# Triangular inverses in blocks of 8, and vector work handed to GpSimd and ScalarE, in a decoder trunk on one core

## The chip, the cores and the metric

One core of a Trainium2 chip. The metric is the device time of one execution in microseconds (us). The engines are PE (TensorE; PEld its weight loads), DVE (VectorE), ACT (ScalarE), POOL (GpSimd) and SP (SyncE, which here only issues transfers). Each engine works through its own instructions in the order in which the program holds them; an instruction that waits holds up all behind it on that engine.

## The reference, cut to what matters

One layer of a hybrid decoder: 2064 prompt tokens (16 learned ones and 2048) and 8 short sample sequences pass through one wide input projection, a gated delta rule (8 heads of 128), an RWKV-7 recurrence (16 heads of 64), two output projections, a gated merge and a last projection. Both recurrences are computed in chunks of 64 tokens. For each chunk and head the kernel needs the inverse of a unit lower triangular 64x64 matrix:

```
lower = where(strict, einsum('bnhik,bnhjk->bnhij', k_beta, k) * decay, 0)
t_inv = triangular_solve(eye + lower, eye, left_side=True, lower=True)
u = einsum('bnhij,bnhjv->bnhiv', t_inv, v_beta)
...
v_new = u_c - w_c @ s ;  o = (q_c * exp(gc)) @ s + qk_c @ v_new
s = s * exp(g_last) + k_tail^T @ v_new          # chunk after chunk
```

## The kernel before, in words

The 33 chunks are cut into 5 segments of 6, 6, 7, 7 and 7 chunks. A segment has 12 units, 4 pairs of delta-rule heads (G) and 8 pairs of RWKV heads (R), so there are 60 units in all. A unit projects its columns (`proj`: 24 matmuls a column block, with each fp32 operand split into a high part and a low rest, both of type fp32r), prepares its chunk matrices (`g_g2`, `g_r2`), inverts them (`g_inv`) and walks through its chunks (`g_g3`, `g_r3`).

`g_inv` goes in two steps. The diagonal 16x16 blocks of all chunks of a unit (48 or 56 of them, one to a partition) are sent through DRAM (`ex`) into the tile `iM`. A second tile, `iD`, is filled with identities by a transfer from `in_consts`. DVE then solves the blocks row by row: row i needs a product of i x i elements into `iT` and a sum along it into row i of `iD`, 15 rows, 30 instructions that each need the one before. GpSimd copies the transpose, the blocks go back through DRAM (`bk`) into `Dn` and `Dt`, and PE combines the 16x16 blocks to 64x64 (`ps_n`, `Z`). `iM`, `iD` and `iT` have one buffer each.

Weights: on first use (segment 0 and the first microseconds of the next), `w_half` loads 128x512 raw weights (`wr`), ACT casts the high part (`wh`), and DVE or GpSimd, in turn by half, subtracts for the rest (`wl`); both parts are stored in DRAM and only loaded from there later on. `split` does the same to an activation before a sum over partitions (`colsum`): `sh` is the high copy and `sl` the rest.

The order of all instructions is made by the kernel itself before anything runs. It records every operation with its dependencies and a planned cost, and a list scheduler (`Sched`) plays a plan in which each engine takes its ready operation of highest rank (`pick`: the chunk walk first, then what touches PSUM, then the rest). `replay` writes that order out, so every instruction carries the source line of `replay` (L903 before, L905 after), and tiles tell them apart. The plan is not corrected at run time: where a transfer lands later than planned, the instruction that needs it stands where the plan put it and its engine stands with it.

Of the kernel before, what the change touches and what calls it, by code (L numbers as in the profile page):

```python
# [4 lines left out]
F32 = mybir.dt.float32  # L5
# [3 lines left out]
ALU = mybir.AluOpType  # L9
AX = mybir.AxisListType  # L10
# [3 lines left out]
D = 1024  # L14
# [11 lines left out]
TS = 4  # L26
NS = NSEQ * TS
SEGMAX = 7
NT = 30
ND = 24  # L30
INFLIGHT = 5
# [10 lines left out]
CONST_LAYOUT = {}  # L42
# [85 lines left out]
def plan(seq):  # L128
    nch = (seq + NM + 63) // 64
    nseg = (nch + SEGMAX - 1) // SEGMAX  # L130
    base, extra = divmod(nch, nseg)
    segs, c0 = [], 0
    pad = nch * 64 - seq - NM
    for i in range(nseg):
        n = base + (1 if i >= nseg - extra else 0)
        t0, t1 = c0 * 64, (c0 + n) * 64
        p = max(0, pad - t0)
        segs.append(dict(i=i, nch=n, T=n * 64, pad=p, nreal=n * 64 - p, r0=max(t0 - pad, 0), last=False, smp=(i == 0)))
        c0 += n
    segs[-1]["last"] = True  # L140
    return segs
# [764 lines left out]
class Trunk:  # L906
# [55 lines left out]
    def split(self, x, n):  # L962

        h, l = self.tr("sh"), self.tr("sl")
        self.nc.vector.tensor_copy(h[:, :n], x)
        self.tt(l[:, :n], x, h[:, :n].bitcast(F32), ALU.subtract)
        return h, l

# [14 lines left out]
    def w_half(self, key):  # L983


        sync = self.nc.sync
        v = lambda x: x.rearrange("p (k n) -> p k n", n=128)
        wh, wl = self.w_tile(F32R, "wh"), self.w_tile(F32R, "wl")
        if key in self.w_dr:
            for w, d in zip((wh, wl), self.w_dr[key]):  # L990
                sync.dma_start(w.bitcast(F32), v(d))
        else:
            raw = self.w_tile(F32, "wr")
            sync.dma_start(raw, v(self.I["wt"][key[0], key[1]]))
            self.nc.scalar.copy(wh, raw)
            self.tt(wl, raw, wh.bitcast(F32), ALU.subtract, self.nc.gpsimd if key[1] else self.nc.vector)
            self.w_dr[key] = [self.p_dr.tile([128, 512], F32, name=f"w{q}_{key[0]}_{key[1]}", tag=f"w{q}_{key[0]}_{key[1]}") for q in "hl"]
            for w, d in zip((wh, wl), self.w_dr[key]):
                sync.dma_start(v(d), w.bitcast(F32))
        return wh, wl  # L1000
# [23 lines left out]
    def setup(self):  # L1024
        nc, I = self.nc, self.I
        P = self.p_c
        nc.scalar.preload_act_table_set("natural_log_exp_and_others")
        self.eps = P.tile([128, 4], F32, name="eps")
        nc.vector.memset(self.eps[:, 0:1], EPS)
        nc.vector.memset(self.eps[:, 1:2], GN_EPS)  # L1030
        nc.vector.memset(self.eps[:, 2:3], 1.0)
        nc.vector.memset(self.eps[:, 3:4], -2.4260151319598084)
        self.consts = P.tile([128, CONST_ON], F32, name="consts")
        nc.sync.dma_start(self.consts[:, 0:128], I["consts"][:, 0:128])

    def g_setup(self):
        nc, I = self.nc, self.I
        P = self.p_c
# [43 lines left out]
        self.abd = [self.dr([128, 8, 40], "abd") for _ in range(2)]  # L1082
        nc.sync.dma_start(self.abd[0], abH.bitcast(F32))
        nc.sync.dma_start(self.abd[1], abL.bitcast(F32))
        self.wbd = [P.tile([128, 2, 128], F32, name=f"wbd{i}") for i in range(1)]
        self.xo = [P.tile([128, 2, 64], F32, name=f"xo{i}") for i in range(2)]
        for w in self.wbd + self.xo:
            nc.gpsimd.memset(w, 0.0)
        self.GS = [P.tile([128, 128], F32, name=f"gs{h}") for h in range(8)]
# [279 lines left out]
    def g_inv(self, sg, u):  # L1369

        nc = self.nc
        n = sg["nch"]
        ex, Nt = u.pop("ex"), u.pop("Nt")
        NB = 8 * n
        M = self.p_i.tile([128, 16, 16], F32, tag="iM", name="iM", bufs=1)
        nc.sync.dma_start(M[:NB], ex)
        Dk = self.p_i.tile([128, 2, 16, 16], F32, tag="iD", name="iD", bufs=1)
        io = CONST_LAYOUT["ID16"][0]
        nc.sync.dma_start(Dk[:NB, 0].rearrange("p a b -> p (a b)"), self.I["consts"][:NB, io:io + 256])
        yield  # L1380
        nc.vector.tensor_scalar(M[:NB], M[:NB], -1.0, None, ALU.mult)
        tmp = self.p_i.tile([128, 16, 16], F32, tag="iT", name="iT", bufs=1)
        for i in range(1, 16):
            a = M[:NB, 0:i, i].unsqueeze(1).to_broadcast([NB, i, i])
            b = Dk[:NB, 0, 0:i, 0:i].rearrange("p m c -> p c m")
            self.tt(tmp[:NB, 0:i, 0:i], a, b, ALU.mult)
            nc.vector.tensor_reduce(Dk[:NB, 0, i, 0:i], tmp[:NB, 0:i, 0:i], AX.X, ALU.add)
            if i % 4 == 3:
                yield
        nc.gpsimd.tensor_copy(Dk[:NB, 1], Dk[:NB, 0].rearrange("p a b -> p b a"))  # L1390
        yield
        bk = self.dr([8 * n, 2, 16, 16], "bk")
        nc.sync.dma_start(bk, Dk[:NB])
        for w, dst in ((0, self.Dn), (1, self.Dt)):
            d3 = dst.rearrange("p (c i) -> p c i", i=64)
            for hf in range(2):
                for b in range(4):
                    q = (hf * 4 + b) * n
                    r = hf * 64 + b * 16
                    nc.sync.dma_start(d3[r:r + 16, 0:n, 16 * b:16 * b + 16], bk[q:q + n, w].rearrange("c j i -> j c i"))  # L1400
        yield
        T = n * 64

        c3 = lambda x: x[:, 0:T].rearrange("p (c t) -> p c t", t=64)

        def quad(lhs, rhs, j=0):

            ps = self.ps("n")
            for c in range(n):
                for hf in range(2):  # L1410
                    r = slice(64 * hf, 64 * hf + 64)
                    k = slice(64 * c + j, 64 * c + 64)
                    self.mm(ps[r, k], lhs[r, 64 * c:64 * c + 64], rhs[r, k])
            return ps

        ps = quad(Nt, self.Dn)
        yield
        Wp = self.t("Wp")
        nc.scalar.copy(Wp[:, :T], ps[:, :T])
        Z = self.t("Z")  # L1420
        nc.gpsimd.tensor_copy(c3(Z)[:, :, 0:16], c3(self.Dt)[:, :, 0:16])
        yield

        for it in range(1, 4):
            j = 16 * it
            ps = quad(Wp, self.Dt if it == 1 else Z, j)
            yield
            self.tt(c3(Z)[:, :, j:], c3(self.Dt)[:, :, j:], c3(ps)[:, :, j:], ALU.subtract)
            yield
        u["U"] = Z  # L1430


    def g_g2(self, sg, p, u):
        nc = self.nc
        T, last, n = sg["T"], sg["smp"], sg["nch"]
        h0 = 2 * p
        W = T + (NS if last else 0)
        GT, cv = sg["GT"], u["cv"]
# [4 lines left out]
        E3 = EP[:, 0:T].rearrange("p (c t) -> p c t", t=64)  # L1443
# [7 lines left out]
        for hh in range(2):  # L1451
            EG = self.t("EG")
            nc.sync.dma_start(EG[:, 0:W], sg["gcd"][h0 + hh:h0 + hh + 1, 0:W].to_broadcast([128, W]))
            sq = {}
# [15 lines left out]
            self.act(EG[:, :W], EG[:, :W], AF.Exp)  # L1470
            if hh == 0:

                self.tt(E3, E3, GT[:, :n, p].unsqueeze(2).to_broadcast([128, n, 64]), ALU.subtract)
                self.tt(E3, E3, self.cst("MNEG").unsqueeze(1).to_broadcast([128, n, 64]), ALU.add, nc.gpsimd)
                self.act(EP[:, 0:T], EP[:, 0:T], AF.Exp)
            yield
            gl = self.sm([128, SEGMAX + 8], "gl", 6)
# [4 lines left out]
            for si, kind in enumerate("kq"):  # L1482
                x = cv[kind, hh]
# [16 lines left out]
        for c0 in range(0, n, 4):  # L1500
            m = min(4, n - c0)
# [23 lines left out]
        for c0 in range(0, n, 4):  # L1525
            m = min(4, n - c0)
# [9 lines left out]
    def g_g3(self, sg, p, u):  # L1536
        nc = self.nc
# [6 lines left out]
        for c in range(n):  # L1544
            k = slice(64 * c, 64 * c + 64)
            g = self.ps("g")
            pr, po, pc = g[:, 0:128], g[:, 128:256], g[:, 256:512]
            for hh in range(2):
                self.mm(pr[H[hh]], kt["k", hh][:, k], S[hh])
            yield  # L1550
            R = self.sm([128, 128], "gR")
            self.tt(R, vt[:, c], pr, ALU.subtract)
            yield
            for hh in range(2):
                self.mm(pr[H[hh]], U[H[hh], k], R[H[hh]])
            yield
            w = self.wbd[0]
            nc.scalar.copy(w[H[0], 0], pr[H[0]])
            nc.vector.tensor_copy(w[H[1], 1], pr[H[1]])
            yield  # L1560
            for hh in range(2):
                self.mm(po[H[hh]], kt["q", hh][:, k], S[hh], start=True, stop=False)
                self.mm(po[H[hh]], KE[:, c, 1], w[:, hh], start=False, stop=True)
            nc.cut(False)
            self.mm(pc, ktl[:, c], w.rearrange("p h v -> p (h v)"))
            yield
            for hh in range(2):
                self.stt(S[hh], S[hh], u["gl", hh][:, c:c + 1], pc[:, 128 * hh:128 * hh + 128], ALU.mult, ALU.add)
            nc.scalar.copy(oS3[:, c], po)
            sq = self.sm([128, 128], "osq", 1)  # L1570
            self.act(sq, oS3[:, c], AF.Square, accum_out=rs[:, c:c + 1])
            yield
# [4 lines left out]
        for c0 in range(0, n, 4):  # L1577
            m = min(4, n - c0)
# [350 lines left out]
    def g_r3(self, sg, p, u):  # L1929
# [5 lines left out]
        H = [slice(0, 64), slice(64, 128)]  # L1935
        AL = u["AL"]
        y = self.t("y")
        xo = self.xo[p % 2]

        nc.scalar.copy(X[H[0], 0, 0], S[H[0]])  # L1940
        nc.vector.tensor_copy(X[H[1], 0, 1], S[H[1]])
# [399 lines left out]
```

## Time and profile before

| | |
|---|---|
| median of 3 runs (lowest, highest) | 4353.93 us (4351.48, 4364.67) |
| profiled execution, its own time | 4371.86 us |
| its span (first to last instruction) | 4370.1 us |
| PE busy | 4066.9 us, 93% |
| DVE busy | 2726.3 us, 62% |
| ACT busy | 1965.2 us, 45% |
| POOL busy | 992.3 us, 23% |
| mean granted TensorE clock | 0.941 |

The profiled execution took 17.9 us more than the median of the runs. Busy time is the union of an engine's instructions; the rest of the span it stood idle. The granted clock is the share of full speed that TensorE was allowed, 1.0 or 0.5 at any moment. Most instructions come from one line, so groups are read by tile: `iT<-iM,iD` writes tile iT from iM and iD.

### The profile page before, as it was taken

What the parts mean: (1) busy time and instruction counts of PE and PEld (TensorE: products, weight loads), DVE (VectorE), ACT (ScalarE), POOL (GpSimd) and SP (SyncE); (2) the same over time, 40 slices, a digit from 0 to 9 for tenths busy, and PEclk for the clock granted to TensorE, in tenths of its full rate; (3) what the DMA queues carried; (4) which work ended last, traced back from release to release, by engine and by line L of the source; (5) the groups of instructions that cost most, each with busy time, mean ns of one, the idle gap of its engine ahead of it and who ended that gap; (6) DMA issues with size and microseconds to landing.
All of it is one profiled execution on the core that took longest, in us unless ns stands there. A gap on an engine that the chain in (4) does not pass through costs nothing. (4 is left out here: it accounts for less than half of the span.)

```text
span 4370.1 us, 91290 instructions
## 1 busy us (share of the span) xinstructions
PE 4066.9 (93%) x32684; PEld 3485.0 (80%) x32684; DVE 2726.3 (62%) x7052; ACT 1965.2 (45%) x4842; POOL 992.3 (23%) x1972
## 2 busy tenths in 40 slices
PE   6888999888999999999999999998998999999998
PEld 6767777778888888888788889787887887778887
DVE  6888677756576754557666645676763456666622
ACT  6544444525444443445444433554443334554431
POOL 3434233413121121212212121121121112111210
PEclk9889788979999999999999999999999999999999
DMA  7636465758745456864445567544445775444467
GB/s 254 201 117 203 136 199 172 243 171 279 235 145 154 137 166 211 263 201 148 126 127 157 172 223 261 159 139 131 128 151 170 237 239 151 128 140 137 143 221 256
DMA packets 660688, 790.09 MB, mean 181 GB/s; under 512 B 251105, under 2 KB 347209, under 8 KB 660234
## 3 DMA queue, kind: packets, MB, share of 16 engines
q1 hardware_dynamic: 660234, 784.25, 57.5%
q8 instruction: 259, 4.24, 0.4%
q14 instruction: 195, 1.60, 0.1%
HBM read 602.29 MB, written 180.56 MB: 179 GB/s over the span
## 5 line engine op out<-in xcount | busy, mean ns | idle before, releaser
L903 PE MATMUL ps_p<-hHL,wh 128*128 128x448 f32 (+3 forms) x7760 | 1828.1, 373 | 30.7 <-ACT wh L903 10.3
L903 PEld LDWEIGHTS ps_p<-hHL,wh 128*128 128x128 f32 x7760 | 1421.3, 195 | 156.1 <-issue 28.3
L903 PE MATMUL ps_p<-hHL,wl 128*128 128x448 f32 (+3 forms) x3880 | 911.6, 358 | 4.9 <-DVE wl L903 2.9
L903 PEld LDWEIGHTS ps_p<-hHL,wl 128*128 128x128 f32 x3880 | 730.2, 193 | 39.0 <-DVE wl L903 3.7
L903 POOL COPY xo<-X 64x64 f32<-64x64 f32 x528 | 172.4, 327 | 809.6 <-ACT X L903 380.1
L903 DVE TENSOR_TENSOR iT<-iM,iD 56x1 f32<-56x1 f32 (+1 forms) x900 | 295.5, 328 | 75.0 <-DMA iD<-in_consts 58.5
L903 ACT COPY raw<-ps_p 128x448 f32<-128x448 f32 (+3 forms) x285 | 144.2, 506 | 343.2 <-PE ps_p L903 313.8
L903 DVE SCALAR_TENSOR_TENSOR cv<-raw,pv,cv 128x448 f32<-128x448 f32 (+1 forms) x360 | 259.3, 720 | 56.0 <-ACT cv L903 48.6
L903 DVE TENSOR_REDUCE iD<-iT 56x1 f32<-56x1 f32 (+1 forms) x900 | 205.1, 228 | 17.7
L903 POOL TENSOR_TENSOR wl<-wr,wh 128x512 fp32r<-128x512 f32 x105 | 149.0, 1419 | 212.0 <-ACT wh L903 137.5
L903 ACT ACTIVATE X<-ps_c 64x64 f32<-64x64 f32 x264 | 55.5, 216 | 289.0 <-PE ps_c L903 124.2
L903 ACT CAST wh<-wr 128x512 fp32r<-128x512 f32 x210 | 128.3, 613 | 77.6 <-DMA wr<-in_wt 21.8
L903 ACT ACTIVATE X<-ps_c,dc 64x64 f32<-64x64 f32 x224 | 68.7, 307 | 207.2 <-DVE X L903 106.4
L903 DVE TENSOR_SCALAR X<-ps_c,dc 64x64 f32<-64x64 f32 x224 | 64.9, 291 | 135.0 <-PE ps_c L903 98.0
L903 ACT ACTIVATE sig<-cv 128x448 f32<-128x448 f32 (+2 forms) x120 | 67.3, 561 | 177.7 <-DVE cv L903 175.9
L903 PE MATMUL ps_p<-mhl,wh 128*128 128x448 f32 (+2 forms) x640 | 141.5, 359 | 5.7 <-ACT wh L903 4.5
L903 DVE TENSOR_SCALAR X<-ps_c 64x64 f32<-64x64 f32 x264 | 58.8, 227 | 131.1 <-PE ps_c L903 88.9
L903 DVE TENSOR_TENSOR Z<-Dt,ps_n 128x336 f32<-128x336 f32 (+1 forms) x180 | 66.9, 372 | 115.5 <-PE ps_n L903 100.0
L903 PE MATMUL ps_g<-gs,cv 128*64 128x128 f32 x1056 | 122.2, 308 | 17.0 <-DVE wbd L903 8.4
L903 PEld LDWEIGHTS ps_n<-Z,Wp 64*64 64x64 f32 x3168 | 109.9, 143 | 24.8 <-issue 9.5
L903 PE MATMUL ps_a<-RH,LH 64*128 64x128 f32 x1056 | 129.3, 292 | 0.0
L903 PE MATMUL ps_n<-Z,Wp 64*64 64x16 f32 (+1 forms) x3168 | 120.3, 220 | 7.7 <-DVE Z L903 5.8
(337 smaller groups left out, 7444.1 us busy)
## 6 DMA issues: line engine op xcount, KB each, us to landing
wh<-wh SPq DMA_DIRECT2D x1050, 256.0 KB
wl<-wl SPq DMA_DIRECT2D x1050, 256.0 KB
wr<-in_wt SPq DMA_DIRECT2D x210, 256.0 KB
gl<-gt SPq DMA_DIRECT2D x72, 224.0 KB
gt<-gt SPq DMA_DIRECT2D x48, 224.0 KB
xt<-in_x_prompt SPq DMA_DIRECT2D x29, 256.0 KB
xt<-in_x_prompt SPq DMA_DIRECT2D x13, 512.0 KB
out_y_p<-xt SPq DMA_DIRECT2D x26, 256.0 KB
```

Source lines behind the costliest of these rows:

```text
L903: getattr(getattr(nc, eng), name)(*[g(x) for x in a], **{q: g(x) for q, x in k.items()})
```

## The change

- `g_inv` solves the two diagonal 8x8 blocks of each 16x16 block side by side, in 7 rows instead of 15, and gets the 8x8 block below them from two matrix products, each in two halves of 256 elements (product into `iT`, sum into the new tile `iX` or into `iD`): 22 DVE instructions instead of 30.
- The identity in `iD` is written by two memsets on GpSimd; the 60 transfers from `in_consts` are gone.
- The negation of `iM`, which is the first to wait for the transfer from `ex`, goes from DVE to GpSimd, as a multiplication by a column of -1.
- In `g_g2` the first operation on `EP` (which waits for a transfer) goes from DVE to GpSimd, and the second, of the same size, from GpSimd to DVE.
- `w_half` subtracts on GpSimd for every half: 105 subtractions of 128x512 change from DVE to GpSimd.
- `split` makes the high copy on ACT: 240 casts change from DVE to ACT.
- `SMP`, `NXO` and `NWB` name numbers that keep their values.

```diff
     def split(self, x, n):
-        self.nc.vector.tensor_copy(h[:, :n], x)
+        self.nc.scalar.copy(h[:, :n], x)
...
-            self.tt(wl, raw, wh.bitcast(F32), ALU.subtract, self.nc.gpsimd if key[1] else self.nc.vector)
+            self.tt(wl, raw, wh.bitcast(F32), ALU.subtract, self.nc.gpsimd)
...
-        nc.sync.dma_start(Dk[:NB, 0].rearrange("p a b -> p (a b)"), self.I["consts"][:NB, io:io + 256])
+        nc.gpsimd.memset(D0, 0.0)
+        nc.gpsimd.memset(D0[:, 0:256:17], 1.0)
         yield
-        nc.vector.tensor_scalar(M[:NB], M[:NB], -1.0, None, ALU.mult)
+        self.tt(M, M, self.eps[:NB, 4:5].unsqueeze(2).to_broadcast([NB, 16, 16]), ALU.mult, nc.gpsimd)
-        for i in range(1, 16):
-            a = M[:NB, 0:i, i].unsqueeze(1).to_broadcast([NB, i, i])
-            b = Dk[:NB, 0, 0:i, 0:i].rearrange("p m c -> p c m")
-            self.tt(tmp[:NB, 0:i, 0:i], a, b, ALU.mult)
-            nc.vector.tensor_reduce(Dk[:NB, 0, i, 0:i], tmp[:NB, 0:i, 0:i], AX.X, ALU.add)
+        for i in range(1, 8):
+            for_a = M2[:, :, 0:i, i].unsqueeze(2).to_broadcast([NB, 2, i, i])
+            for_b = D2[:, :, 0:i, 0:i].rearrange("p h m c -> p h c m")
+            tv = tmp[:NB, 0:2, 0:i, 0:i]
+            self.tt(tv, for_a, for_b, ALU.mult)
+            nc.vector.tensor_reduce(D2[:, :, i, 0:i], tv, AX.X, ALU.add)
...
+        for q in range(2):
+            tv = tmp[:NB]
+            self.tt(tv, M[:, 0:8, 8 + 4 * q:12 + 4 * q].rearrange("p m i -> p i m").unsqueeze(2).to_broadcast([NB, 4, 8, 8]),
+                    D[:, 0:8, 0:8].rearrange("p m c -> p c m").unsqueeze(1).to_broadcast([NB, 4, 8, 8]), ALU.mult)
+            nc.vector.tensor_reduce(Xt[:NB, 4 * q:4 * q + 4], tv, AX.X, ALU.add)
...
+        for q in range(2):
+            tv = tmp[:NB]
+            self.tt(tv, D[:, 8 + 4 * q:12 + 4 * q, 8:16].unsqueeze(2).to_broadcast([NB, 4, 8, 8]),
+                    Xt[:NB].rearrange("p m c -> p c m").unsqueeze(1).to_broadcast([NB, 4, 8, 8]), ALU.mult)
+            nc.vector.tensor_reduce(D[:, 8 + 4 * q:12 + 4 * q, 0:8], tv, AX.X, ALU.add)
...
-                self.tt(E3, E3, GT[:, :n, p].unsqueeze(2).to_broadcast([128, n, 64]), ALU.subtract)
-                self.tt(E3, E3, self.cst("MNEG").unsqueeze(1).to_broadcast([128, n, 64]), ALU.add, nc.gpsimd)
+                self.tt(E3, E3, GT[:, :n, p].unsqueeze(2).to_broadcast([128, n, 64]), ALU.subtract, nc.gpsimd)
+                self.tt(E3, E3, self.cst("MNEG").unsqueeze(1).to_broadcast([128, n, 64]), ALU.add)
```

The costs that the scheduler plans with are the same, but the operations have other engines, so the whole order is made anew. Two places show it. The first is where the first inverse of the program starts on DVE. Before (kb and cv belong to other units' preparation; sh and sl are high copy and rest):

```order
L903 TENSOR_SCALAR iM<-iM 48x256
L903 CAST sh<-kb 128x416
L903 COPY rVs<-ps_a 64x128
L903 COPY rBKs<-ps_a 64x128
L903 TENSOR_TENSOR iT<-iM,iD 48x1
L903 TENSOR_TENSOR sl<-kb,sh 128x416
L903 TENSOR_REDUCE iD<-iT 48x1
```

and in the changed kernel:

```order
L905 TENSOR_TENSOR iT<-iM,iD 48x2
L905 TENSOR_TENSOR LH<-kb,cs 64x6x64
L905 TENSOR_REDUCE iD<-iT 48x2
L905 TENSOR_TENSOR rLs<-ta,cs 128x32
L905 TENSOR_TENSOR iT<-iM,iD 48x2x2x2
L905 TENSOR_TENSOR rLs<-kb,cs 128x32
L905 TENSOR_REDUCE iD<-iT 48x2x2
```

The negation and the cast have left DVE; the first product still stands in DVE's order and needs iM, which now comes out of GpSimd. The second place is GpSimd in segment 0, about when the first units are prepared. Before (carA, rs, cvo and raw are small copies and memsets around the projections, V a product, gl a column of decays):

```order
L903 TENSOR_TENSOR V<-cv,sig 128x6x64
L903 TENSOR_TENSOR wl<-wr,wh 128x512
L903 COPY carB<-raw 128x1
L903 MEMSET raw 128x52
L903 COPY gl<-EG 128x6
L903 COPY gl<-EG 128x8
L903 TENSOR_TENSOR wl<-wr,wh 128x512
```

and in the changed kernel:

```order
L905 TENSOR_TENSOR V<-cv,sig 128x6x64
L905 MEMSET iD 48x272
L905 TENSOR_TENSOR wl<-wr,wh 128x512
L905 MEMSET iD 48x16
L905 MEMSET raw 128x52
L905 TENSOR_TENSOR wl<-wr,wh 128x512
L905 COPY carA<-raw 128x3
L905 COPY rs<-raw 128x8x4
L905 TENSOR_TENSOR wl<-wr,wh 128x512
```

Twice as many weight subtractions stand between GpSimd's small copies, and the memsets of iD beside them.

## Rows read from the trace of the kernel before

**Rows 1.** The page, part 1: busy us, share of span, instructions.

```profile
PE 4066.9 (93%) x32684; PEld 3485.0 (80%) x32684; DVE 2726.3 (62%) x7052; ACT 1965.2 (45%) x4842; POOL 992.3 (23%) x1972
```

**Rows 2.** Span and mean granted TensorE clock of the core.

```profile
core 0: 4370.1 us, clock 0.941
```

**Rows 3.** Stretches: us, busy PE, PEld, DVE, ACT, POOL, clock, DMA share, GB/s.

```profile
109.00:437.00 328.00, 277.34 (x2151) 234.18 (x2149) 273.33 (x739) 159.75 (x376) 127.76 (x240) 0.86 0.56 174
...
1110.00:4370.00 3260.00, 3105.27 (x25146) 2665.76 (x25144) 1947.95 (x5055) 1446.69 (x3587) 619.64 (x1303) 0.96 0.56 174
```

**Rows 4.** What PE waited for: total us, times, longest us.

```profile
PE ps_c L903 <- DVE X L903: 26.9, 22, 4.3
...
PE ps_p L903 <- POOL wl L903: 0.7, 1, 0.7
...
PE ps_a L903 <- DVE SVT L903: 0.2, 1, 0.2
```

**Rows 5.** What DVE waited for, transfers only.

```profile
DVE iM L903 <- DMA iM<-ex: 69.8, 25, 9.3
DVE iT L903 <- DMA iD<-in_consts: 58.5, 13, 5.6
DVE EP L903 <- DMA EP<-gcd: 41.5, 11, 9.4
```

**Rows 6.** What POOL waited for, its longest transfer.

```profile
POOL Z L903 <- DMA Dt<-bk: 158.0, 36, 9.3
```

**Rows 7.** Timeline near 3730 us: start, us, instruction, [idle before <- releaser].

```profile
3729.29 0.15 DVE L903 TENSOR_TENSOR iT<-iM,iD 56x1 f32<-56x1 f32 x1 [5.57 <-DMA iD<-in_consts]
...
3731.41 0.49 PE L903 MATMUL ps_c<-xo,consts 128*64 128x64 f32 x4 [4.30 <-DVE X L903]
```

**Rows 8.** Timeline of PE, five idle stretches behind DVE.

```profile
451.40 0.57 PE L903 MATMUL ps_a<-sX,KM 32*128 32x128 f32 x1 [2.78 <-DVE soT L903]
...
568.94 0.41 PE L903 MATMUL ps_a<-consts,vt 128*128 128x128 f32 x2 [1.11 <-DVE KM L903]
...
649.20 0.42 PE L903 MATMUL ps_a<-consts,rv 128*64 128x128 f32 x1 [1.56 <-DVE iD L903]
...
3656.56 0.47 PE L903 MATMUL ps_g<-gR,Z 64*64 64x128 f32 x2 [4.96 <-DVE gR L903]
...
3991.73 0.58 PE L903 MATMUL ps_g<-gs,cv 128*64 128x128 f32 x3 [0.86 <-DVE wbd L903]
```

**Rows 9.** Groups by tile: instruction, count | busy us, mean ns | idle before.

```profile
L903 DVE TENSOR_TENSOR iT<-iM,iD 56x1 f32<-56x1 f32 (+1 forms) x900 | 295.5, 328 | 75.0 <-DMA iD<-in_consts 58.5
L903 DVE TENSOR_REDUCE iD<-iT 56x1 f32<-56x1 f32 (+1 forms) x900 | 205.1, 228 | 17.7
...
L903 POOL TENSOR_TENSOR wl<-wr,wh 128x512 fp32r<-128x512 f32 x105 | 149.0, 1419 | 212.0 <-ACT wh L903 137.5 <-PE ps_p L903 24.9 <-DMA wh<-wh 10.3
```

**Rows 10.** The same by shape, DVE.

```profile
L903 DVE TENSOR_TENSOR wl<-wr,wh 128x512 fp32r<-128x512 f32 x105 | 80.8, 770 | 27.3 <-DMA wl<-wl 10.7 <-ACT wh L903 9.4 <-DMA wh<-wh 3.0
L903 DVE CAST sh<-sq 128x448 fp32r<-128x448 f32 x72 | 31.5, 437 | 14.3 <-ACT sq L903 12.2 <-PE ps_a L903 1.6
...
L903 DVE TENSOR_TENSOR iT<-iM,iD 56x100 f32<-56x100 f32 x36 | 11.9, 330 | 0.7
...
L903 DVE TENSOR_TENSOR iT<-iM,iD 48x100 f32<-48x100 f32 x24 | 11.0, 460 | 0.4
...
L903 DVE TENSOR_TENSOR iT<-iM,iD 56x1 f32<-56x1 f32 x36 | 5.4, 149 | 35.7 <-DMA iD<-in_consts 35.2
...
L903 DVE TENSOR_REDUCE iD<-iT 56x1 f32<-56x1 f32 x36 | 5.2, 143 | 0.9
```

**Rows 11.** The same by shape, ACT, the nearest cast.

```profile
L903 ACT CAST hHL<-hHL 128x448 fp32r<-128x448 f32 x48 | 25.3, 564 | 31.1 <-DMA hHL<-oB 30.3 <-DMA hHL<-oA 0.5
```

**Rows 12.** Timeline near 370 us, POOL and DVE.

```profile
369.83 1.36 POOL L903 TENSOR_TENSOR wl<-wr,wh 128x512 fp32r<-128x512 f32 x1
...
369.99 1.38 DVE L903 TENSOR_TENSOR iT<-iM,iD 48x100 f32<-48x100 f32 x1
```

More of the change, by code (lines that the diff above doesn't have):

```diff
@@ L28 @@
 SEGMAX = 7
+SMP = 0
+NXO, NWB = 2, 1
 NT = 30
@@ L137, in plan @@
         p = max(0, pad - t0)
-        segs.append(dict(i=i, nch=n, T=n * 64, pad=p, nreal=n * 64 - p, r0=max(t0 - pad, 0), last=False, smp=(i == 0)))
+        segs.append(dict(i=i, nch=n, T=n * 64, pad=p, nreal=n * 64 - p, r0=max(t0 - pad, 0), last=False, smp=(i == SMP)))
         c0 += n
@@ L1027, in setup @@
         nc.scalar.preload_act_table_set("natural_log_exp_and_others")
-        self.eps = P.tile([128, 4], F32, name="eps")
+        self.eps = P.tile([128, 8], F32, name="eps")
         nc.vector.memset(self.eps[:, 0:1], EPS)
@@ L1031, in setup @@
         nc.vector.memset(self.eps[:, 2:3], 1.0)
+        nc.vector.memset(self.eps[:, 4:5], -1.0)
         nc.vector.memset(self.eps[:, 3:4], -2.4260151319598084)
@@ L1084, in g_setup @@
         nc.sync.dma_start(self.abd[1], abL.bitcast(F32))
-        self.wbd = [P.tile([128, 2, 128], F32, name=f"wbd{i}") for i in range(1)]
-        self.xo = [P.tile([128, 2, 64], F32, name=f"xo{i}") for i in range(2)]
+        self.wbd = [P.tile([128, 2, 128], F32, name=f"wbd{i}") for i in range(NWB)]
+        self.xo = [P.tile([128, 2, 64], F32, name=f"xo{i}") for i in range(NXO)]
         for w in self.wbd + self.xo:
@@ L1374, in g_inv @@
         NB = 8 * n
[L1375 to L1378, printed above, removed]
-        nc.sync.dma_start(Dk[:NB, 0].rearrange("p a b -> p (a b)"), self.I["consts"][:NB, io:io + 256])
-        yield
-        nc.vector.tensor_scalar(M[:NB], M[:NB], -1.0, None, ALU.mult)
-        tmp = self.p_i.tile([128, 16, 16], F32, tag="iT", name="iT", bufs=1)
@@ L1383, in g_inv @@
-        for i in range(1, 16):
-            a = M[:NB, 0:i, i].unsqueeze(1).to_broadcast([NB, i, i])
-            b = Dk[:NB, 0, 0:i, 0:i].rearrange("p m c -> p c m")
-            self.tt(tmp[:NB, 0:i, 0:i], a, b, ALU.mult)
-            nc.vector.tensor_reduce(Dk[:NB, 0, i, 0:i], tmp[:NB, 0:i, 0:i], AX.X, ALU.add)
+        PB = 272
+        Mt = self.p_i.tile([128, PB], F32, tag="iM", name="iM", bufs=1)
+        sq = lambda x: x[:, 0:256].rearrange("p (a b) -> p a b", b=16)
+        dg = lambda x: x.rearrange("p (h x) -> p h x", x=136)[:, :, 0:128].rearrange("p h (a b) -> p h a b", b=16)
@@ new lines, in g_inv @@
+        M = sq(Mt[:NB])
+        nc.sync.dma_start(M, ex)
+        Dt_ = self.p_i.tile([128, 2, PB], F32, tag="iD", name="iD", bufs=1)
+        D0 = Dt_[:NB, 0]
+        nc.gpsimd.memset(D0, 0.0)
+        nc.gpsimd.memset(D0[:, 0:256:17], 1.0)
+        yield
+        self.tt(M, M, self.eps[:NB, 4:5].unsqueeze(2).to_broadcast([NB, 16, 16]), ALU.mult, nc.gpsimd)
+        tmp = self.p_i.tile([128, 4, 8, 8], F32, tag="iT", name="iT", bufs=1)
+        Xt = self.p_i.tile([128, 8, 8], F32, tag="iX", name="iX", bufs=1)
@@ L1388, in g_inv @@
+        M2, D2 = dg(Mt[:NB]), dg(D0)
+        for i in range(1, 8):
[4 more added lines that the diff above has]
+            nc.vector.tensor_reduce(D2[:, :, i, 0:i], tv, AX.X, ALU.add)
             if i % 4 == 3:
                 yield
-        nc.gpsimd.tensor_copy(Dk[:NB, 1], Dk[:NB, 0].rearrange("p a b -> p b a"))
+        D = sq(D0)
@@ new lines, in g_inv @@
+        for q in range(2):
[3 more added lines that the diff above has]
+            nc.vector.tensor_reduce(Xt[:NB, 4 * q:4 * q + 4], tv, AX.X, ALU.add)
+        yield
+        for q in range(2):
[3 more added lines that the diff above has]
+            nc.vector.tensor_reduce(D[:, 8 + 4 * q:12 + 4 * q, 0:8], tv, AX.X, ALU.add)
@@ L1391, in g_inv @@
+        nc.gpsimd.tensor_copy(sq(Dt_[:NB, 1]), D.rearrange("p a b -> p b a"))
         yield
         bk = self.dr([8 * n, 2, 16, 16], "bk")
-        nc.sync.dma_start(bk, Dk[:NB])
+        nc.sync.dma_start(bk.rearrange("p w a b -> p w (a b)"), Dt_[:NB, :, 0:256])
         for w, dst in ((0, self.Dn), (1, self.Dt)):
@@ L1556, in g_g3 @@
             yield
-            w = self.wbd[0]
+            w = self.wbd[p % NWB]
             nc.scalar.copy(w[H[0], 0], pr[H[0]])
@@ L1937, in g_r3 @@
         y = self.t("y")
-        xo = self.xo[p % 2]
+        xo = self.xo[p % NXO]
         nc.scalar.copy(X[H[0], 0, 0], S[H[0]])
```

## The prediction

> **What bounds the kernel now.** I read the busy shares first, then the granted clock, then what PE waited for, then what those it waited for had themselves waited for. PE is busy for 4066.9 of 4370.1 us [rows 1], so it sets the end, and nothing in this change removes work from it. What can be won is its idle time, 303.2 us, and what comes with it: the clock was granted at 0.941 on average [rows 2], so (1 - 0.941) x 4370 = 258 us of full-speed time were lost to the lower level. It is lost where PE idles: in 109 to 437 us, where PE stands still 15% of the time, the clock is 0.86, and after 1110 us, where it stands still 5%, 0.96 [rows 3]. A microsecond of idle PE therefore costs at most (303 + 258) / 303 = 1.85 us. Some of the low clock lies over idle time and costs nothing twice, so I reckon with 1.6.
>
> In PE's waits 38 rows name DVE; the first and the last stand in [rows 4], and together they are 196.0 us in 124 waits, two thirds of the idle time. DVE itself is not full (62%), so the question is why it is late. In three rows it waits for a transfer: for `iM`, for `iD` and for `EP`, 69.8, 58.5 and 41.5 us [rows 5]. Everything behind the waiting instruction is held up, the chunk walk too: near 3730 us DVE stands 5.57 us before the first product of an inverse, because the identity of `iD` has not landed, and PE stands 4.30 us until the `X` behind it [rows 7]. I followed each of the 124 waits back along DVE's unbroken run to the idle time in which that run began. It is the wait for `iD` in 11 cases with 26.5 us of idle PE (from 649.20 to 3731.41 us), the one for `iM` in 17 with 36.2 us (568.94 to 3991.73), the one for `EP` in 8 with 32.9 us (451.40 to 3656.56); the first and last of each kind stand in [rows 7, 8]. That leaves 100.4 us in which DVE was late for other reasons.
>
> **The change part by part.** *Identity by memset.* The 60 transfers go, and with them the wait in [rows 7]. Without it the 26.5 us of idle PE are worth 26.5 x 1.6 = 42 us. But the memset must itself wait until the blocks of the inverse before have been sent from `iD`, so a late inverse still delays the next one; I take two thirds, 28 us, with ends 0 and 42.
>
> *Blocks of 8.* Before, 900 products take 295.5 us and 900 sums 205.1 us [rows 9], over 60 x 1240 = 74,400 elements a partition. The smallest ones take 149 and 143 ns [rows 10]; with these as fixed parts the rest is (295.5 - 134.1) / 74,400 = 2.17 ns an element for the products and (205.1 - 128.7) / 74,400 = 1.03 ns for the sums. After, there are 660 of each over 60 x (2 x 140 + 4 x 256) = 78,240 elements: 98 + 170 and 94 + 81, together 443 us instead of 501. With the negation gone as well, DVE is spared some 60 to 75 us; I reckon with 70.
>
> *High copies on ACT.* 240 casts leave DVE, at 437 ns for the commonest [rows 10]: 105 us. ACT does such a cast in 564 ns [rows 11], so it takes on 135 us and goes from 45% to 48%. The copy there follows the square on ACT itself in most cases, so no hand-over is added. I put 0 on ACT, with an end of 20 us on the slow side, since its queue also empties PSUM for PE.
>
> *What 175 us less on DVE are worth.* They are 6.4% of its 2726.3 us, spread over the whole span, so only those behind which PE waits count. Of the 100.4 us a cut in proportion would be 6 us; a run that is all casts and inverse could lose everything. I take 20 us, times 1.6: 32 us, with ends 10 and 100.
>
> *Low weight parts.* 105 subtractions, 80.8 us, leave DVE [rows 10] and cost GpSimd 1419 ns each, 149 us [rows 9], nearly all before 1110 us. There DVE is the fuller one: 273.33 of 328 us in 109 to 437 us [rows 3]. But the two engines hold each other up. At 369.99 us a product of 48x100 that starts inside a GpSimd subtraction takes 1.38 us and ends with it [rows 12]; the same product averages 460 ns in the two segments of 6 chunks, the first of which has the subtractions, and 330 ns in those of 7 [rows 10]. If each of the 105 catches DVE halfway, it holds it 0.65 us, 68 us in all: DVE gains 81 - 68 = 13 us, which I count as nothing. The ends are no hold (81 us off DVE; half of it at PE, 40 us gained) and a full hold of 1419 ns each, which costs DVE 149 - 81 = 68 us. The Trainium skill (GPSIMD Engine Reference, section 1, Specifications) says that GpSimd's SBUF interfaces are shared with VectorE and contended for by VectorE instructions with two SBUF inputs. By that page alone, which gives no duration, the move would be worth anything between those two ends; the lengthened product above agrees with it. The same skill (Perfetto Trace Analysis, section Optimizing Scalar/DVE Operations) warns that moving operations between those two might not help; by this the term is zero, as taken.
>
> *Waits moved to GpSimd.* `EP` and `iM` now wait there. But DVE's next operation needs the result: the addition on `EP` and the first product of the inverse both follow in DVE's order as soon as the plan thinks GpSimd done. A transfer that is 5 us late makes GpSimd 5 us late and DVE with it. What is won is only what GpSimd's queue adds to the plan between the two. I take a tenth of (36.2 + 32.9) x 1.6 = 111 us, 11 us; the ends are 0 and 111. Behind the waiting GpSimd instruction stand the small copies of the chunk walk (`xo`) and of the projections; DVE and ACT wait for these. GpSimd already waits 158.0 us for one kind of transfer [rows 6], and PE waits for GpSimd's `wl` only once, 0.7 us [rows 4], so I put no price on that.
>
> The sum: 28 + 32 + 0 + 11 = 71 us. From the profiled execution's 4371.9 us this gives 4301 us; that execution lies 17.9 us over the median of the runs, 4353.9 us, from which I predict 4283 us.
>
> **The rivals.** *GpSimd becomes the late one in segment 0 (slower).* It holds twice the weight subtractions, each behind ACT's cast and so behind a transfer, and its memsets and copies for the projections stand among them. For it: 1419 ns against 770 makes each of the 105 halves 0.65 us later, and DVE is held meanwhile. Against it: PE waits 0.7 us for `wl` from GpSimd today [rows 4]. If all of it reached PE, 105 x 0.65 x 1.6 = 109 us would be added, against 71 won: 4354 + 38 = 4392 us. It decides from about 44 us of idle PE on, that is when two thirds of the 105 come too late. The full hold of every subtraction, 68 us on DVE and from there on PE, would come to the same 68 x 1.6 = 109 us; it is what the Trainium skill's rule of the shared interfaces (GPSIMD Engine Reference, section 1, Specifications) would make of this at its worst.
>
> *The stalls only change their names (no change).* DVE waits for GpSimd where it waited for transfers, and the order made anew puts other instructions behind them. For it: the dependencies just described, and DVE's relief of 6.4% falls mostly where PE doesn't wait. Against it: the wait for `iD` has no successor of its length. 4354 us.
>
> *GpSimd takes the waits up (more is gained).* If GpSimd's queue gives DVE enough room in the plan, half of the 111 us go instead of a tenth, 45 us more: 4238 us. All of it would be 4183 us. For it: GpSimd idles 77% and its own long waits rarely reach PE. Against it: the direct dependency.
>
> **How the numbers follow.** Forecast 0.55, more gained 0.20, no change 0.14, slower 0.11. The time is that of the forecast, 4283 us; its own range, by the ends of the DVE relief (10 to 60 of its 100) and the identity (0 to 42), is 4240 to 4333. The range that should hold 8 in 10 takes in most of the bigger gain and the no-change case and ends short of the full slower one: 4195 to 4375. Less than 0.3%, 13 us, can't be told from no change here; the three runs of before lie 13.2 us apart. Forecast and bigger gain are faster, 0.75; same 0.14; slower 0.11.
>
> **What would show it.** No DVE wait for a transfer into `iD`, and none of 4 to 6 us before the first product of an inverse that isn't `iM`'s. DVE busy near 2540 us, ACT near 2100, POOL near 1200. DVE still waits for GpSimd's `iM` and `EP`, together some 80 us or more; if these are short, the bigger gain is right. In segment 0 DVE's busy share stays above 75%, and its two-input operations get longer. PE idle falls from 303 to about 260 us and the clock rises to about 0.95. The prediction is wrong if PE waits for GpSimd's `wl` or `raw` for tens of microseconds, or if the order made anew has long stalls in places that this trace doesn't show.

## The result and the profile after

The changed kernel takes 4288.82 us (median of 4 runs, 4281.86 to 4305.56), the kernel before 4359.30 us (4 runs, 4351.48 to 4366.08). The ratio is 0.9845, interval 0.9807 to 0.9882: faster by 70 us. 4283 us were predicted, and the sum of 71 us looks exact. The experiments below show that its terms are not. One run of all, of the kernel with only DVE's load changed, took 6393.49 us at a granted clock of 0.688 and is left out of that kernel's time and ratio.

The page of the changed kernel, busy times as in [rows 1], and its span and clock as in [rows 2]:

```profile
PE 4023.9 (94%) x32684; PEld 3439.8 (80%) x32684; DVE 2565.5 (60%) x6168; ACT 2068.5 (48%) x5082; POOL 1178.1 (28%) x2257
```

```profile
core 0: 4280.1 us, clock 0.958
```

PE idles 4280.1 - 4023.9 = 256.2 us, 47 us less than before, and the span is 90.0 us shorter: a microsecond of idle time was worth 1.9 us here, or 1.5 us by the 70 us between the medians, since the profiled execution before was a long one. The stretches of the changed kernel (columns as in [rows 3]), and behind them the stretch of the kernel before that isn't among those:

```profile
109.00:437.00 328.00, 275.74 (x2171) 232.54 (x2169) 250.89 (x629) 163.88 (x398) 164.02 (x280) 0.84 0.52 157
437.00:983.00 546.00, 503.91 (x4477) 426.40 (x4477) 374.41 (x879) 267.58 (x672) 248.98 (x373) 0.93 0.65 210
```

```profile
437.00:983.00 546.00, 500.31 (x4295) 413.40 (x4295) 358.88 (x956) 230.76 (x592) 166.31 (x279) 0.84 0.58 184
```

Segment 0, up to 437 us, won next to nothing. From 437 to 983 us the clock rose from 0.84 to 0.93, and 4477 matmuls fit where 4295 did. This stretch stands in no row ahead of the prediction: before, PE stood still in it for 8% of the time, less than the 15% of 109 to 437 us, and yet had the lower clock, 0.84 to 0.86.

What DVE waited for after the change (total us, times, longest; compare [rows 5]), and then POOL and PE:

```profile
DVE sl L905 <- ACT sh L905: 83.4, 63, 10.0
...
DVE iT L905 <- POOL iM L905: 53.5, 26, 7.0
...
DVE EP L905 <- POOL EP L905: 11.5, 7, 2.5
```

```profile
POOL iM L905 <- DMA iM<-ex: 84.0, 34, 7.2
...
POOL iD L905 <- DMA bk<-iD: 49.7, 29, 7.6
```

```profile
PE ps_p L905 <- POOL wl L905: 4.3, 4, 1.8
```

The wait for the identity is gone, those for `iM` and `EP` have become waits for GpSimd, 65.0 us instead of 111.3. A new one is the longest of the three: DVE waits 83.4 us for the high copies `sh` that ACT now makes. The groups of the inverse in the changed kernel (columns as in [rows 9]):

```profile
L905 DVE TENSOR_TENSOR iT<-iM,iD 56x2 f32<-56x2 f32 (+1 forms) x540 | 184.7, 342 | 67.7 <-POOL iM L905 53.5 <-POOL E L905 3.8
L905 DVE TENSOR_REDUCE iD<-iT 56x2 f32<-56x2 f32 (+1 forms) x540 | 126.3, 234 | 11.0
L905 DVE TENSOR_TENSOR iT<-iD,iX 56x256 f32<-56x256 f32 (+1 forms) x120 | 84.7, 706 | 2.1
L905 DVE TENSOR_REDUCE iX<-iT 56x32 f32<-56x256 f32 (+1 forms) x120 | 48.8, 407 | 1.9
```

The four groups sum to 444.5 us, where 443 were worked out from [rows 9, 10].

### The profile page after: what moved, and what is told of

Read it like the earlier page. It is cut to its first block, busy times and chain, and to the rows that moved or that the text cites. A ratio compares the mean times of both kernels' runs of the same rounds, so it can differ in the third digit from the quotient of the medians.

```text
span 4280.1 us, 90570 instructions
## 1 busy us (share of the span) xinstructions
PE 4023.9 (94%) x32684; PEld 3439.8 (80%) x32684; DVE 2565.5 (60%) x6168; ACT 2068.5 (48%) x5082; POOL 1178.1 (28%) x2257
## 4 chain that ended last, share of the span: by engine, by line
PE 74%; DVE 9%; DMA 7%; ACT 3%; SPq 3%; issue 2%; POOL 1%; DVEq 0%; POOLq 0%; ACTq 0%
PE ps_p L905 50%; PE ps_a L905 10%; PE ps_c L905 5%; PE ps_g L905 5%; PE ps_n L905 4%; SPq L905 3%; DVE cv L905 1%; DVE iT L905 1%; DMA wl<-wl 1%; DMA EG<-gcd 1%; DMA bk<-iD 1%; DVE LH L905 1%; DMA wr<-in_wt 1%; DMA wh<-wh 1%; DMA EP<-gcd 1%
## 5 line engine op out<-in xcount | busy, mean ns | idle before, releaser
L905 POOL TENSOR_TENSOR wl<-wr,wh 128x512 fp32r<-128x512 f32 x210 | 288.6, 1376 | 186.9 <-ACT wh L905 100.7
L905 DVE TENSOR_TENSOR iT<-iM,iD 56x2 f32<-56x2 f32 (+1 forms) x540 | 184.7, 342 | 67.7 <-POOL iM L905 53.5
L905 POOL COPY carB<-raw 128x1 f32<-128x1 f32 x132 | 33.0, 251 | 389.4 <-ACT raw L905 380.2
L905 PE MATMUL ps_g<-gs,cv 128*64 128x128 f32 x1056 | 120.2, 304 | 20.6 <-DVE gs L905 7.2
L905 DVE TENSOR_TENSOR gl<-gl,ps_p 128x448 f32<-128x448 f32 (+2 forms) x80 | 47.2, 590 | 146.5 <-PE ps_p L905 135.3
L905 DVE TENSOR_REDUCE iD<-iT 56x2 f32<-56x2 f32 (+1 forms) x540 | 126.3, 234 | 11.0
```

Of the source, the lines that this page charges most:

```text
L905: getattr(getattr(nc, eng), name)(*[g(x) for x in a], **{q: g(x) for q, x in k.items()})
```

## The experiments

My theory was the prediction's: the identity and DVE's relief are worth most of it. The rivals: only the relief counts; only the moved waits count; or none of the parts does, and the order made anew is simply a better one. In the ratios below the kernel before is 1; the medians of before beside these runs lie between 4359.04 and 4362.53 us.

**The same work in another order.** First a control: the planner's fixed cost of a DVE instruction is raised from 160 to 163 ns, in both kernels. The work stays the same, only the plan, and with it the order on every engine, comes out different.

```diff
-                d = N / 0.96 + 160
+                d = N / 0.96 + 163
```

In the kernel before: 

> The kernel before with the same work on the same engines; only the planner's fixed cost of a DVE instruction is 163 instead of 160 ns, so that the order is made anew. Waits and load theories: no change, within 0.3% of 4359 us. Order theory (the gain of the change is a luckier order): more than 15 us away from 4359 us, either way.

Measured: 4297.9 us, ratio 0.9865 (0.9848 to 0.9883). The old kernel in another order wins 59 us, nearly as much as the whole change.

In the changed kernel: 

> The changed kernel with the same re-made order (163 instead of 160 ns). Waits and load theories: 4289 us within 0.3%, that is 0.984 of before. Order theory: it loses a good part of the 71 us, over 4315 us.

Measured: 4315.56 us, ratio 0.9903 (0.9888 to 0.9917), 25 us more than the changed kernel by the ratios.

**Half of the change, planned anew.** The kernel before with the three edits that move waits (memset, negation and first `EP` operation on GpSimd):

```diff
-        nc.sync.dma_start(Dk[:NB, 0].rearrange("p a b -> p (a b)"), self.I["consts"][:NB, io:io + 256])
+        nc.gpsimd.memset(Df, 0.0)
+        nc.gpsimd.memset(Df[:, 0:256:17], 1.0)
...
-        nc.vector.tensor_scalar(M[:NB], M[:NB], -1.0, None, ALU.mult)
+        self.tt(M[:NB], M[:NB], minus_one, ALU.mult, nc.gpsimd)
...
-                self.tt(E3, E3, GT[...], ALU.subtract)
-                self.tt(E3, E3, MNEG, ALU.add, nc.gpsimd)
+                self.tt(E3, E3, GT[...], ALU.subtract, nc.gpsimd)
+                self.tt(E3, E3, MNEG, ALU.add)
```

(Here and below `minus_one` and `MNEG` stand for the constants, written out in the kernel as broadcast columns.)

> The kernel before with only the waits moved: identity by memset, negation of iM and first operation on EP on GpSimd. Waits theory (what was gained is PE's idle time behind DVE's waits for transfers, 26.5 us for iD and 46 of the 69 us for iM and EP, times 1.6): about the whole gain, 4280 to 4300 us. Load theory, the prediction's own sum: 28 + 11 us, about 4320 us. Order theory: anything.

Measured: 4314.51 us, ratio 0.9899 (0.9874 to 0.9924). The other half, blocks of 8 and casts on ACT, with the identity by transfer, the negation and `EP` on DVE and `wl` by turns:

> The kernel before with only DVE's load changed: blocks of 8 and high copies on ACT; the waits and the low weight parts stay where they were. Waits theory: no change, 4350 to 4365 us. Load theory, the prediction's own sum: 32 us less, about 4327 us, with 10 to 100 us possible. Order theory: anything.

Measured: 4296.95 us (median of four runs), ratio 0.9864 (0.9843 to 0.9885). Both halves win 1.0 to 1.4%, and so does the control in which nothing changes. Nothing can be read from either.

**How far orders scatter.** Two more plans for each kernel, with 157 and 166 ns in the line above.

> The kernel before, same work, order re-made with a planned DVE cost of 157 instead of 160 ns. The control with 163 ns gave 4298 us, so the order alone can be worth 60 us. Order theory (before's own order at 160 ns is an unlucky one, and the change has no gain of its own): 4290 to 4320 us. Gain theory (the change is worth about 70 us in any order): this lies 50 to 80 us over the changed kernel at 157 ns. Middle: 20 to 40 us over it.

Measured: 4289.69 us, ratio 0.9830 (0.9809 to 0.9850).

> The same with 166 ns. Order theory: 4290 to 4320 us, as the changed kernel. Gain theory: 50 to 80 us over the changed kernel at 166 ns. Middle: 20 to 40 us over it.

Measured: 4380.44 us, ratio 1.0045 (1.0029 to 1.0061).

> The changed kernel, order re-made with 157 ns. Order theory: 4290 to 4320 us, no lower than before at 157 ns. Gain theory: 4275 to 4300 us. Middle: 20 to 40 us under before at 157 ns.

Measured: 4240.36 us, ratio 0.9718 (0.9699 to 0.9738), the fastest kernel of this study, 49 us under before at 157 ns and below the range of either theory.

> The changed kernel, order re-made with 166 ns. Order theory: 4290 to 4320 us, no lower than before at 166 ns. Gain theory: 4275 to 4300 us. Middle: 20 to 40 us under before at 166 ns.

Measured: 4272.47 us, ratio 0.9788 (0.9771 to 0.9806).

| fixed cost in the plan | 157 | 160 | 163 | 166 | mean |
|---|---|---|---|---|---|
| kernel before | 0.9830 | 1 | 0.9865 | 1.0045 | 0.9935 |
| changed kernel | 0.9718 | 0.9845 | 0.9903 | 0.9788 | 0.9814 |

Four orders of the same work differ by 2.15% before and 1.85% after; the standard deviations are 45 and 34 us. The means differ by 0.0121, 53 us, with a standard error of 28 us (each deviation squared, divided by 4, summed, root). So the change is likely worth something, about as much as it showed, but less than two standard errors is not proof, and one pair of kernels could not have told: with 163 ns the changed one is the slower of the two.

What the prediction aimed at shows more clearly than the time. PE's idle time behind DVE, summed over its waits as in [rows 4], and all its other idle time, from the profiled executions (us):

| fixed cost in the plan | 157 | 160 | 163 | 166 | mean |
|---|---|---|---|---|---|
| before: behind DVE | 139.8 | 195.9 | 156.6 | 165.1 | 164.4 |
| before: other | 121.2 | 107.2 | 100.6 | 143.3 | 118.1 |
| changed: behind DVE | 96.2 | 121.3 | 122.1 | 94.8 | 108.6 |
| changed: other | 127.6 | 134.9 | 155.8 | 145.5 | 141.0 |

In every order of the changed kernel PE idles less behind DVE than in any order of the old one, by 56 us in the mean; some 23 of these come back as other waits. The mean clock of the changed kernels is 0.956 to 0.962, that of the old ones 0.941 to 0.950.

**One term at a time, order held.** The last four runs keep the plan of the kernel before, and with it the order on PE, row by row. Only when the order is written out is the chosen operation issued in another form, at its old place in the sequence.

```diff
             g = lambda x: x.real() if isinstance(x, V) else x
+            if "as_" in k:
+                k["as_"](nc, [g(x) for x in a])
+                continue
```

*The identity alone:*

```diff
-        nc.sync.dma_start(..., self.I["consts"][:NB, io:io + 256])
+        nc.sync.dma_start(..., self.I["consts"][:NB, io:io + 256],
+                          as_=lambda nc, a: (nc.gpsimd.memset(a[0], 0.0), nc.gpsimd.memset(a[0][:, 0:256:17], 1.0)))
```

> The order of every engine is that of the kernel before; alone the identity of iD is written by two GpSimd memsets at the place where its transfer was issued. The prediction's term: 28 us less (0 to 42), a ratio of 0.9936 (0.990 to 1.0), DVE's wait for a transfer into iD gone, and PE's idle time some 17 us less at full price for the clock. Rival, the stall is passed on because the memset itself waits for the blocks of the inverse before: DVE then waits for GpSimd's iD for 30 us or more, the ratio is over 0.997.

Measured: 4298.32 us (6 runs), ratio 0.9857 (0.9832 to 0.9881): 62 us won, interval 52 to 73. The page of this kernel:

```profile
PE 4032.6 (94%) x32684; PEld 3458.2 (81%) x32684; DVE 2725.1 (63%) x7052; ACT 1967.4 (46%) x4842; POOL 1011.3 (24%) x2092
```

and the large memsets in its groups by shape on POOL:

```profile
L1383 POOL MEMSET iD<- 56x256 f32 x36 | 11.0, 307 | 19.7 <-DMA bk<-iD 19.5
...
L1383 POOL MEMSET iD<- 48x256 f32 x24 | 7.6, 315 | 4.9 <-DMA bk<-iD 4.6 <-POOL carB L906 0.2
```

The span is 4294.9 us, so PE idles 262.3 us, 40.9 less than before. GpSimd waits 24.1 us until the old blocks are sent, but no product of an inverse waits for GpSimd's `iD`; the longest wait of any DVE instruction for it is 3.0 us. The stall was not passed on. This is the price in one order, that of the kernel before.

*`iM` and `EP` alone:*

```diff
-        nc.vector.tensor_scalar(M[:NB], M[:NB], -1.0, None, ALU.mult)
+        self.tt(M[:NB], M[:NB], minus_one, ALU.mult, as_=lambda nc, a: nc.gpsimd.tensor_tensor(*a))
...
-                self.tt(E3, E3, GT[...], ALU.subtract)
-                self.tt(E3, E3, MNEG, ALU.add, nc.gpsimd)
+                self.tt(E3, E3, GT[...], ALU.subtract, as_=lambda nc, a: nc.gpsimd.tensor_tensor(*a))
+                self.tt(E3, E3, MNEG, ALU.add, nc.gpsimd, as_=lambda nc, a: nc.vector.tensor_tensor(*a))
```

> Order of before held; the first operation on EP and the negation of iM are done by GpSimd, the second on EP by DVE, each at its old place. The prediction's view is that without a new order the wait is only renamed: within 5 us of before, a ratio of 0.999 to 1.001, or up to 15 us slower, since a GpSimd negation takes longer than DVE's and DVE stands behind it. Rival (GpSimd takes the waits up): at least half of 111 us goes, a ratio of 0.987 or less. DVE's waits for GpSimd's iM and EP together about as long as its waits for these transfers were, 111 us, by the first; under 60 by the second.

Measured: 4364.12 us (12 runs), ratio 1.0006 (0.9991 to 1.0021). What DVE waited for in it:

```profile
DVE iT L906 <- POOL iM L1385: 64.0, 26, 8.7
...
DVE EP L1478 <- POOL EP L1477: 32.9, 12, 6.5
```

Together 96.9 us, where the waits for the transfers were 111.3 [rows 5]. Without a new order the wait only changes its name.

*Blocks of 8 and casts on ACT.* The 22 new instructions of the inverse stand at the places of the first 22 old ones, the last 8 are left out; the negation stays on DVE, and the sums between the two products go into a corner of `iM` that is no longer needed, not into a tile `iX`.

```diff
-        self.nc.vector.tensor_copy(h[:, :n], x)
+        self.nc.vector.tensor_copy(h[:, :n], x, as_=lambda nc, a: nc.scalar.copy(*a))
...
+            self.tt(tmp[:NB, 0:i, 0:i], a, b, ALU.mult,
+                    as_=lambda nc, a, s=s: s and nc.vector.tensor_tensor(s[0].real(), s[1].real(), s[2].real(), ALU.mult))
```

> Order of before held; the inverse in blocks of 8 with two products and the 240 high casts on ScalarE, at the places of the old ones. DVE's busy time falls by 150 to 180 us in any case. The prediction's term: 32 us less (10 to 100), ratio 0.9927 (0.977 to 0.998). Rival from the remade orders, in which the share of PE's idle time with other reasons did not fall: within 10 us of before, 0.9977 to 1.0023. Second rival: ScalarE's longer queue costs PE up to 20 us, a ratio up to 1.005.

Measured: 4386.45 us (9 runs), ratio 1.0051 (1.0035 to 1.0068): 22 us lost, although DVE is busy for 136 us less (150 to 180 were expected). The page of this kernel:

```profile
PE 4083.1 (93%) x32684; PEld 3480.9 (79%) x32684; DVE 2590.7 (59%) x6332; ACT 2074.3 (47%) x5082; POOL 973.2 (22%) x1972
```

and the wait on DVE that is new in it, with the two longest that the same high copies had on DVE before:

```profile
DVE sl L906 <- ACT sh L968: 84.1, 90, 5.9
```

```profile
DVE sh L903 <- ACT ysq L903: 23.1, 20, 3.2
DVE sh L903 <- ACT sq L903: 13.8, 17, 2.2
```

PE idles 302.0 us (span 4385.1), as before: of the 136 us that DVE saves, much goes into waiting for ACT. On PE this hand-over shows neither as gain nor as loss: PE's own waits for `sh` and `sl` sum to 30.5 us before and 28.8 here, those for ACT in all to 64.6 and 69.7. So the second rival, whose time this nearly is, isn't the reason. The loss is that PE is 16.2 us longer busy, at a clock of 0.944 that is no lower. The wide matmuls of the projections, the kernel before and this one (durations in ns: shortest, median, longest):

```profile
L903 PE MATMUL ps_p<-hHL,wh x7760: 324/362/935, 37.9 to 4315.7; 128*128 128x448 f32 x119, 128*128 128x384 f32 x40, 128*128 128x368 f32 x25, 128*128 128x376 f32 x15
L903 PE MATMUL ps_p<-hHL,wl x3880: 323/360/578, 40.6 to 4316.5; 128*128 128x448 f32 x116, 128*128 128x384 f32 x39, 128*128 128x368 f32 x26, 128*128 128x376 f32 x13
```

```profile
L906 PE MATMUL ps_p<-hHL,wh x7760: 323/365/935, 37.1 to 4330.5; 128*128 128x448 f32 x119, 128*128 128x384 f32 x40, 128*128 128x368 f32 x25, 128*128 128x376 f32 x15
L906 PE MATMUL ps_p<-hHL,wl x3880: 323/365/689, 39.8 to 4331.3; 128*128 128x448 f32 x116, 128*128 128x384 f32 x39, 128*128 128x368 f32 x26, 128*128 128x376 f32 x13
```

The medians rise by 3 and 5 ns, the means by 1.4 and 2.0 (372.5 to 373.9, 357.5 to 359.5). It is not the same for all: by width, the median of 448 columns goes from 363 to 366, that of 384 from 336 to 334 and that of 368 from 330 to 329. By groups of the whole run it is 1840.3 instead of 1828.1 us and 920.0 instead of 911.6, 20.6 us in all, about what was lost.

*All low weight parts on GpSimd:*

```diff
-            self.tt(wl, raw, wh.bitcast(F32), ALU.subtract, self.nc.gpsimd if key[1] else self.nc.vector)
+            self.tt(wl, raw, wh.bitcast(F32), ALU.subtract, self.nc.gpsimd if key[1] else self.nc.vector, as_=lambda nc, a: nc.gpsimd.tensor_tensor(*a))
```

> Order of before held; all 210 low weight parts on GpSimd, where before every second was on DVE. The prediction's term is nothing: within 13 us of before, 0.997 to 1.003. Rival (GpSimd late in segment 0, or holding DVE): slower by 38 to 109 us, a ratio of 1.009 to 1.025, most of it before 1110 us, with PE waiting for GpSimd's wl or behind longer DVE products. Other rival: DVE gains its 81 us and half reach PE, 40 us less, 0.991.

Measured: 4379.87 us (12 runs), ratio 1.0033 (1.0019 to 1.0047): 14 us lost. Its page:

```profile
PE 4069.9 (93%) x32684; PEld 3487.7 (80%) x32684; DVE 2714.3 (62%) x6947; ACT 1967.1 (45%) x4842; POOL 1120.3 (26%) x2077
```

and PE's wait for GpSimd, 0.7 us before [rows 4]:

```profile
PE ps_p L906 <- POOL wl L999: 6.6, 6, 2.0
```

DVE lost 80.8 us of work [rows 10] and is busy for only 12.0 us less: its remaining instructions are busy 68.8 us longer. Their order is the same in both runs, so they can be compared one by one: the 427 that overlap a subtraction on GpSimd take 75.4 us longer, the other 6520 together 15.2 us less. GpSimd holds DVE up. PE idles 5.8 us more, as much as the new wait for `wl`.

## Why the prediction came out right, and where it was not

The total was right, and so were most marks that were named for it: DVE busy for 2565.5 us (2540 expected), ACT 2068.5 (2100), POOL 1178.1 (1200), 256 us of idle PE (260), no wait into `iD`; only `EP` and `iM` cost DVE 65.0 us instead of 80 or more. The terms behind the total were mostly wrong: two of the four lie outside their own ends, one with the wrong sign, and together they give a third of the gain. That the total fits is luck. Held one at a time, from ratios times 4360.9 us (the median of before beside these runs; negative is faster):

| term | predicted, ends | measured, order held |
|---|---|---|
| identity by memset | -28 (0 to -42) | -62 |
| blocks of 8 and casts (DVE's relief) | -32 (-10 to -100) | +22 |
| low weight parts | 0 (-40 to +109) | +14 |
| `iM` and `EP` to GpSimd | -11 (0 to -111) | +3 |
| sum | -71 | -23 |

*Identity.* The mechanism was right, the size was not. The step that failed is the upper end, 26.5 x 1.6: it took only those idle stretches of PE that trace back to this wait. Held, they went to 0, but PE's idle time fell by 40.9 us. Of the other 14 us, what traces back to `iM` and `EP` gave 4.5 (70.8 to 66.3 us, counting some waits of `EP`, 1.7 us before and 7.2 after, that the trace puts down to other transfers), and PE's own waits for transfers 7.4 (27.4 to 20.0). The cut by a third for a memset that waits was wrong as well: GpSimd had the room. The factor held as a number: 62 / 40.9 = 1.5, or 1.8 by the two profiled spans, where 1.6 was taken. Its reason holds less well: that the low clock lies where PE idles was read from two stretches, and the third, 437 to 983 us, has less idle time than the first and a lower clock.

*DVE's relief.* The step that failed is "I take 20 us" of the 100.4. The work on the inverse fell as worked out, 444.5 us for 443, but not where PE waits for it: of PE's idle time behind DVE, what traces back to other reasons than the three transfers was 100.4 us before, 97.8 in the held run and 99 after the whole change. The 6 us of a cut in proportion was the better guess. That "no hand-over is added" was wrong too: the rest `sl` stays on DVE and reads `sh`. On DVE it came from the same engine; now DVE waits 84.1 us for ACT in the held order and 83.4 in the new one. On the other side the copies no longer wait on DVE for ACT's squares and `y`, 40.5 us before. Whether the relief would have reached PE without this hand-over is not shown: no run had the blocks of 8 with the casts on DVE in the held order.

*The longer matmuls* appear in no term. All six kernels here that have the blocks of 8 and the casts on ACT show medians of 365 and 365 ns, the eight others 362 and 360, in whatever order. In those six the wider `iM` and `iD` push every tile behind them, `hHL` among them, further on in each partition: by 192 bytes in the held one (64 for `iM`, 128 for `iD`), by 448 in the five with the new tile `iX` (256 more). The casts and the blocks of 8 do not do it by running at the same time: the matmuls of 448 columns during which none of either runs, 5465 of 6984 in the held run, have a median of 365 ns, where such ones had 363 before. I take the place of `hHL` to be the cause, but that is argued, not shown: no kernel had the new place without the rest. Wide tiles alone, with the old work, would tell.

*Low weight parts.* The hold on DVE was estimated at 68 us and measured at 68.8; that DVE gains 13 us and PE nothing was nearly so. The Trainium skill (GPSIMD Engine Reference, section 1, Specifications) names the contention of GpSimd with two-input instructions of VectorE without a duration. This run agrees, since instructions with two tensor inputs bear 56.7 of the 60.1 us by which DVE's instructions, added up singly, got longer; and it gives a duration, 68.8 us over 105, some 0.65 us for a subtraction of 128x512. The rival of a late GpSimd had the right sign at an eighth of its price: 6.6 us of waiting reached PE, not 68.

*`iM` and `EP`.* As argued, the dependency hands the wait on: +3 us, interval -4 to +9, with the order held. In the new order PE's idle time behind both fell from 69.1 to some 22 us, so part of the bigger gain came true there, with the new order and not through the edit alone.

*The order.* The terms held singly sum to -23 us, the change measured -70. The rest, some 47 us, comes from the new order or from edits acting together; which of the two stays open. It is no more than orders of the same work differ by. That scatter is what the prediction lacked: it priced terms of 11 to 32 us in a kernel whose order would be made anew, while plans that differ by 3 ns in one cost lie 25 to 78 us apart (neighbours in the table of orders). Its range happened to be wide enough. And before's own order is a poor one of its four: their mean is 0.9935, 28 us less, without any change.

## What to carry to other kernels

Where a program plans its own order, first measure what the same work in two or three other orders does; a difference inside that scatter says nothing about the edit by itself. To price one edit, keep the planned order and swap only the instruction when it is written out. The price holds for that order; another may have another. And of an operation moved to another engine ask not only who feeds it but who reads it next: a pair that followed each other on one engine becomes a wait.

## What was not expected of the hardware

- The wide matmuls of the projections took 362 and 360 ns (medians) in eight kernels, 365 and 365 in the six whose tiles lie 192 or 448 bytes further on, with the same instructions and counts; over 11,640 of them that is 20.6 us between the kernel before and the held one. The cause stays open.
- GpSimd holds DVE up: 105 subtractions moved from DVE to GpSimd, 80.8 us, made DVE only 12.0 us less busy.
- A removed stall of 26.5 us on PE gave back 40.9 us of idle time and 62 us of time: other waits shortened as well, and the share of the span at the lower clock fell with them (mean clock 0.941 before, 0.949 with the identity alone).
